# 144 sixteen-bit products ahead of a down projection, and casts among the up projection, in a two-layer trunk on one core

## The chip, the cores and the metric

The kernel runs on one core of one Trainium2 chip. The time is device microseconds of one launch, the median of several runs. Beside it there is a trace of one execution, taken by the hardware profiler.

## The reference

Two layers over 256 frames of width 1024, each an attention mixer and then a PEER mixer with a layer norm behind each. Layer 0's attention is multi-head latent attention, layer 1's selects 64 keys per query. The change lies in the PEER mixer of layer 0. It picks 16 of 16384 experts for each token and head, and mixes them:

```python
s1 = einsum('thd,hnd->thn', q[:, :, 0], sub_keys[0]);  s2 = ...q[:, :, 1], sub_keys[1]
v1, i1 = top_k(s1, 16);  v2, i2 = top_k(s2, 16)
best, pos = top_k(v1[..., :, None] + v2[..., None, :], 16)   # experts = pairs of keys
gate = softmax(best)
u = w_down[expert];  a = einsum('td,ted->te', x, u)
y = einsum('te,ted->td', gelu(a) * gate, w_up[expert])
x = layernorm(ALPHA * x + y)
```

## The kernel before, in words

The kernel doesn't gather experts. It multiplies all 256 tokens with all 16384 rows of the down table, 128 blocks of 128 experts each, applies gelu, multiplies by a gate that is zero except at the chosen experts, and multiplies the result with all 128 blocks of the up table. Each 32-bit operand is split into a part `hi` and a rest `lo` (the weights) or `xh` and `xl` (the activations), and each product is three: hi with xh, hi with xl, lo with xh.

**The weight stream** (class `Stream`). SyncE loads a block of 128x1024 into one of four `raw` buffers (L101). ScalarE casts it to `hi` (L119), VectorE subtracts to get `lo` (L123; on GpSimd at L121 for some blocks). `hi` and `lo` go into rings of four blocks (`RING = 4`), so a cast waits until TensorE has used the block four before it, and a load waits until the subtraction has freed its buffer.

**`peer(li)`** runs for each layer. `queries` and `scores` make the queries (products `pq`) and their scores against the keys (products `ps`, 32-bit, 128 wide). While they and the first part of the down stage run, `choose` does the top-16 steps on VectorE, dealt out in portions between the products. `gates` ends it, with four transposes on TensorE (`gT`, L1056).

*The down stage* is the loop over `b0`: two blocks per turn, each of 24 products `d` with 256 columns, out of a pool of four PSUM buffers (`ps(...)`, the pool `psp`); ScalarE applies gelu. From the point where the gates are ready, each turn also has `prepare` (16-bit one-hot tables on VectorE L1119, GpSimd L1121 and ScalarE L1125) and `place`, 16 products `G` of 16 bits and 128 columns.

*The up stage* is the loop over `k`: 128 blocks, each of 12 products `y` with 512 columns into four PSUM banks that stay open to the end. Before every second block `operand` splits the activations into `xh` (ScalarE, L1182) and `xl` (VectorE, L1183). At `k == 64` the code asks for the loads of the residual `x` and of the norm's gain and bias, into places of the arena `A` whose activations have been used. `finish` takes the last four blocks and the norm.

All matmuls but the transposes are issued by one helper, so they bear line L277. The tables `iotac` (50x16 entries) and `iota4` (128x4), both 16-bit and filled with small whole numbers, are made at the start; the function `first` already multiplies `iotac` with a 16-bit `iota16`, into a PSUM tile `idle` that nobody reads (L1219), before the first weights have landed.

**What sets the order.** The framework's scheduler puts the instructions of each engine into one fixed order, by a simulation of its own; `chains` and `issue_after` hold some of them in the written order. On the chip each engine takes its queue strictly in that order.

Of the kernel before, what the change touches and what calls it, by code (L numbers as in the profile page):

```python
# [12 lines left out]
F16 = mybir.dt.float16  # L13
U32 = mybir.dt.uint32
AF = mybir.ActivationFunctionType
ALU = mybir.AluOpType
AX = mybir.AxisListType

P = 128
T = 256  # L20
D = 1024
# [162 lines left out]
def tile_trunk(ctx: ExitStack, tc: tile.TileContext, ins, out: bass.AP):  # L184
    nc = tc.nc
# [18 lines left out]
    def ps(name):  # L204
        return psp.tile([P, 512], F32, tag="ps", name=name)
# [15 lines left out]
    iota4 = const.tile([P, P, 4], F16, tag="iota4", name="iota4")  # L221
    iotac = const.tile([P, CELLS, TOPK], F16, tag="iotac", name="iotac")
# [84 lines left out]
    def load_x(ar, src):  # L307
        xs = [ar.take(D), ar.take(D)]
        for t in range(2):
            nc.sync.dma_start(xs[t], src[t])  # L310
        return xs
# [203 lines left out]
    def load_affine(ar, li, which):  # L515
        g, b = ar.take(D), ar.take(D)
        nc.sync.dma_start(g, ins["ln_gain"][li, which].partition_broadcast(P))
        nc.sync.dma_start(b, ins["ln_bias"][li, which].partition_broadcast(P))
        return g, b
# [421 lines left out]
    def peer(li):  # L941
# [186 lines left out]
        def place(g4, done):  # L1128
# [10 lines left out]
            if done:  # L1139
                nc.vector.scalar_tensor_tensor(A[:, :done, tsl], pv[:, :done, :], 1.0 / GSCALE, A[:, :done, tsl],  # L1140
                                               op0=ALU.mult, op1=ALU.mult)

        groups = prepared = 0
        ready = False
        for b0 in range(0, NKEYS, 2):
            p = ps(f"d{b0}")
# [26 lines left out]
        lnar = Arena(arena)  # L1173
# [15 lines left out]
        for k in range(NKEYS - STAGGER):  # L1189
            rows(y4, operand(k), ws.get(), k == 0, False)  # L1190
            if k == 64:
                x = load_x(lnar, keep)
                g, b = load_affine(lnar, li, 1)
        spare = [lnar.take(D) for _ in range(5)]

        finish(y4, operand, NKEYS, g, b, x, spare, None if last else lead_values)

# [66 lines left out]

    mla()
    peer(0)
    dsa()
    peer(1)


# [71 lines left out]
```

## Time and profile before

| | us |
|---|---|
| median of the runs | 1798.12 |
| the two runs | 1797.7 and 1798.54 |
| profiled execution | 1797.2 |
| its span in the trace | 1795.4 |
| down stage of layer 0, from 145.07 to | 529.41 |
| up stage of layer 0, from 529.41 to | 877.60 |
| granted TensorE clock, mean | 0.999 |

The page of the profile has the busy time of each engine and the chain that ended last, followed back from the last instruction. The view of groups has, for each kind of instruction, its count, busy time, the mean time of one, and the idle time ahead of it with what ended it. PE is TensorE, PEld its weight loads, DVE VectorE, ACT ScalarE, POOL GpSimd, SP SyncE. Matmuls overlap in the trace, so the time that one more costs is the distance between starts, which the chain gives as a piece's length over its count.

### The profile page before, as it was taken

The numbers are of one execution on the slowest core, as the hardware profiler recorded it, in microseconds if no ns is written. First come the engines' busy times: TensorE is split into PE (matmuls) and PEld (weight loads), VectorE is DVE, ScalarE is ACT, GpSimd is POOL, SyncE is SP. The second block draws the span as 40 slices with busy tenths as digits, with TensorE's granted clock in tenths as the row PEclk, the third lists the DMA queues.
The fourth block names the chain that finished last, engine by engine and source line by source line (L and its number), as shares of the span: only waits on it lengthen the run. The fifth ranks groups of instructions, "written<-read, shape, count | busy, mean of one in ns | idle before, by whom it ended". The sixth has DMA issues, their size and how long they took to land.

```text
span 1795.4 us, 32370 instructions
## 1 busy us (share of the span) xinstructions
PE 1784.0 (99%) x12495; PEld 1631.1 (91%) x12495; DVE 1336.2 (74%) x2319; ACT 1053.2 (59%) x1832; POOL 406.2 (23%) x288
## 2 busy tenths in 40 slices
PE   9999999999999999999999999999999999999998
PEld 8899999999998888888889899999999988888886
DVE  6688998888985555555688789997889865555555
ACT  6655545888864444444467554557888754444443
POOL 2012354555520000000023013544555400000000
PEclk9999999999999999999999999999999999999999
DMA  6555556444556565655646455565454476565553
GB/s 233 211 175 179 189 200 194 159 165 165 165 188 222 190 198 191 196 191 196 205 164 225 172 173 185 192 200 177 165 164 162 157 246 197 190 197 190 196 191 118
DMA packets 93468, 335.47 MB, mean 187 GB/s; under 512 B 10368, under 2 KB 11392, under 8 KB 93312
## 3 DMA queue, kind: packets, MB, share of 16 engines
q1 hardware_dynamic: 93024, 332.87, 56.0%
q8 instruction: 98, 1.61, 0.3%
q14 instruction: 58, 0.48, 0.1%
q10 hardware_dynamic: 288, 0.52, 0.1%
HBM read 329.16 MB, written 4.19 MB: 186 GB/s over the span
## 4 chain that ended last, share of the span: by engine, by line
PE 98%; DVE 1%; issue 0%; DMA 0%; ACT 0%; POOL 0%; SPq 0%; DVEq 0%; POOLq 0%; ACTq 0%
PE y L277 41%; PE d L277 39%; PE pq L277 4%; PE G L277 3%; PE q L277 3%; PE v L277 1%; PE qw L277 1%; PE s L277 1%; PE ps L277 1%; PE h L277 1%; PE qi L277 1%; PE o L277 1%; PE qn L277 0%; DMA raw<-in_mla_h 0%; PE pt L280 0%
## 5 line engine op out<-in xcount | busy, mean ns | idle before, releaser
L123 DVE TENSOR_TENSOR lo<-raw,hi 128x1024 fp32r<-128x1024 f32 (+1 forms) x556 | 747.5, 1346 | 289.5 <-ACT hi L119 288.0
L119 ACT CAST hi<-raw 128x1024 fp32r<-128x1024 f32 (+1 forms) x583 | 611.0, 1049 | 522.8 <-PE d L277 222.4
L277 PE MATMUL d<-xh,hi 128*128 128x256 f32 x2048 | 572.9, 280 | 0.0
L277 PE MATMUL d<-xh,lo 128*128 128x256 f32 x2048 | 566.8, 277 | 0.0
L277 PE MATMUL d<-xl,hi 128*128 128x256 f32 x2048 | 566.8, 277 | 0.0
L277 PEld LDWEIGHTS d<-xh,lo 128*128 128x128 f32 x2048 | 385.2, 188 | 0.0
L277 PEld LDWEIGHTS d<-xh,hi 128*128 128x128 f32 x2048 | 384.9, 188 | 0.0
L277 PEld LDWEIGHTS d<-xl,hi 128*128 128x128 f32 x2048 | 384.7, 188 | 0.0
L277 PE MATMUL y<-hi,xh 128*128 128x512 f32 x1088 | 337.8, 390 | 0.0
L277 PE MATMUL y<-lo,xh 128*128 128x512 f32 x1088 | 337.7, 389 | 0.0
L277 PE MATMUL y<-hi,xl 128*128 128x512 f32 x1088 | 337.2, 389 | 0.0
L1121 POOL TENSOR_TENSOR gate<-hot,gate 128x512 f16<-128x512 f16 x128 | 220.5, 1741 | 214.4 <-DVE hot L1119 214.4
L277 PEld LDWEIGHTS y<-lo,xh 128*128 128x128 f32 x1088 | 204.1, 188 | 42.8 <-DVE lo L123 0.3
L277 PEld LDWEIGHTS y<-hi,xl 128*128 128x128 f32 x1088 | 204.2, 188 | 42.4
L277 PEld LDWEIGHTS y<-hi,xh 128*128 128x128 f32 x1088 | 203.8, 188 | 41.9
L371 POOL TENSOR_TENSOR st<-st,mhalf 128x1 f32<-128x1 f32 x8 | 4.4, 550 | 802.1 <-DVE st L369 802.1
L1125 ACT ACTIVATE gate<-hot,rest 128x128 f16<-128x128 f16 x512 | 165.9, 411 | 1.1 <-DVE hot L1119 1.0
L1182 ACT CAST xh<-arena 128x512 fp32r<-128x512 f32 x128 | 79.7, 623 | 145.5 <-PE y L277 145.3
L1183 DVE TENSOR_TENSOR xl<-arena,xh 128x512 fp32r<-128x512 f32 x128 | 88.2, 692 | 72.7 <-ACT xh L1182 72.7
L121 POOL TENSOR_TENSOR lo<-raw,hi 128x1024 fp32r<-128x1024 f32 x27 | 65.2, 2414 | 218.4 <-ACT hi L119 213.1
L1119 DVE TENSOR_TENSOR hot<-iota,place 128x1024 f16<-128x1024 f16 x128 | 85.7, 709 | 32.3 <-PE G L277 32.2
L1043 POOL TENSOR_TENSOR arena<-arena 128x800 f32<-128x800 f16 x32 | 71.0, 2229 | 58.1 <-DVE arena L1040 58.1
(220 smaller groups left out, 1803.5 us busy)
## 6 DMA issues: line engine op xcount, KB each, us to landing
raw<-in_down SPq DMA_DIRECT2D x256, 512.0 KB, 3.3
raw<-in_up SPq DMA_DIRECT2D x256, 512.0 KB, 4.3
raw<-in_peer_q SPq DMA_DIRECT2D x24, 512.0 KB, 4.2
raw<-in_dsa_qk SPq DMA_DIRECT2D x16, 512.0 KB, 3.4
raw<-in_mla_w_o SPq DMA_DIRECT2D x8, 512.0 KB, 5.6
arena<-in_peer_q SPq DMA_DIRECT2D x8, 512.0 KB, 5.1
raw<-in_dsa_v SPq DMA_DIRECT2D x8, 512.0 KB, 4.4
raw<-in_dsa_w_o SPq DMA_DIRECT2D x8, 512.0 KB, 4.3
```

Source lines behind the costliest of these rows:

```text
L119: self.act(lambda: nc.scalar.copy(hi, raw))
L121: nc.gpsimd.tensor_tensor(lo, raw, hi.bitcast(F32), op=ALU.subtract)
L123: self.dve(lambda: nc.vector.tensor_tensor(lo, raw, hi.bitcast(F32), op=ALU.subtract))
L277: return pe(lambda: nc.tensor.matmul(o, l, r, start=start, stop=stop, skip_group_check=True))
L371: nc.gpsimd.tensor_tensor(st[:, 5:6], st[:, 4:5], mhalf, op=ALU.pow)
L1043: nc.gpsimd.tensor_tensor(o.rearrange("p k c -> p c k"), same, cell[t][:, h, :, None].to_broadcast([P, CELLS, TOPK]), op=ALU.mult)
L1119: nc.vector.tensor_tensor(hot, iota4[:, None].to_broadcast([P, 2, P, 4]), place16[:, :, None, four].to_broadcast([P, 2, P, 4]), op=ALU.is_ ...
L1121: nc.gpsimd.tensor_tensor(gate[:, 0], hot[:, 1].rearrange("p c j -> p j c"), gate16[:, four, None].to_broadcast([P, 4, P]), op=ALU.mult)
L1125: nc.scalar.mul(gate[:, 1, j, :], hot[:, 1, :, j], rest[:, t : t + 1])
L1182: nc.scalar.copy(hh, a)
L1183: nc.vector.tensor_tensor(al, a, hh.bitcast(F32), op=ALU.subtract)
```

## The change

Two insertions, both for layer 0 only. The first puts 144 products with their own weight loads ahead of the down loop: 96 with 256 columns and 48 with 512, from the tables `iotac` (as weights, at eight offsets) and `iota4`, into a PSUM tile `spin` out of the pool of four. Nobody reads it. The second puts five instructions into the up loop, three times: a 16-bit scaled copy of `x[0]` on ScalarE, the remainder on VectorE, the same again with a sum, and a scaled copy and a remainder on GpSimd. They write to the places `spare`, which `finish` uses later for the norm; `spare` is now taken at `k == 64` instead of behind the loop, at the same addresses.

```diff
+        if li == 0:
+            flat = iotac.rearrange("p c k -> p (c k)")
+            wide4 = iota4.rearrange("p k j -> p (k j)")
+            spin = ps("spin")
+            for width, count in ((256, 96), (512, 48)):
+                for i in range(count):
+                    nc.tensor.matmul(spin[:, :width], flat[:, 80 * (i % 8) : 80 * (i % 8) + P],
+                                     wide4[:, :width], start=True, stop=True)
+
         groups = prepared = 0
         ready = False
         for b0 in range(0, NKEYS, 2):
...
             if k == 64:
                 x = load_x(lnar, keep)
                 g, b = load_affine(lnar, li, 1)
-        spare = [lnar.take(D) for _ in range(5)]
+                spare = [lnar.take(D) for _ in range(5)]
+            if k in (80, 84, 88) and li == 0:
+                hi16, lo16 = spare[0].bitcast(F16)[:, :D], spare[1].bitcast(F16)[:, :D]
+                nc.scalar.mul(hi16, x[0], 1024.0)
+                nc.vector.scalar_tensor_tensor(lo16, x[0], 1024.0, hi16, op0=ALU.mult, op1=ALU.subtract)
+                nc.vector.scalar_tensor_tensor(lo16, x[0], 1024.0, hi16, op0=ALU.mult, op1=ALU.subtract,
+                                               accum_out=spare[2][:, 0:1])
+                nc.gpsimd.tensor_scalar(lo16, x[0], 1024.0, None, op0=ALU.mult)
+                nc.gpsimd.tensor_tensor(lo16, x[0], hi16, op=ALU.subtract)
```

Apart from the insertions the order of every engine is the same as before, but for one place: the second half of the last score products. Before, TensorE's queue has it inside the first down block. Here are the last rows of that stretch, before the change (`d` is the first down block):

```order
L277 MATMUL d_1570<-xh,hi 128x256
L277 MATMUL d_1570<-xl,hi 128x256
L277 MATMUL ps_1558<-arena 128x128 x2
L277 MATMUL ps_1564<-arena 128x128 x2
L277 MATMUL d_1570<-xh,lo 128x256
```

With the change the same four products stand among the new ones, behind 26 of them, as they stood behind 26 of `d`:

```order
L1149 LDWEIGHTS iotac
L1149 MATMUL spin<-iota_99,iotac 128x256
L277 MATMUL ps_1558<-arena 128x128 x2
L277 MATMUL ps_1564<-arena 128x128 x2
L1149 LDWEIGHTS iotac
```

The first down block comes behind the last of the 144. In the queue of VectorE the casts' instructions stand between the subtractions `lo` and `xl` of the up stage, among the early blocks, and not where the code asks for them; the second of the three looks so (`raw_7331` to `raw_7383` are blocks 23 to 26):

```order
L123 TENSOR_TENSOR lo<-raw_7331,hi 128x1024
L123 TENSOR_TENSOR lo<-raw_7349,hi 128x1024
L1207 SCALAR_TENSOR_TENSOR arena<-arena 128x1024
L1192 TENSOR_TENSOR xl<-arena,xh 128x512
L1208 SCALAR_TENSOR_TENSOR arena<-arena 128x1024
L123 TENSOR_TENSOR lo<-raw_7365,hi 128x1024
L123 TENSOR_TENSOR lo<-raw_7383,hi 128x1024
```

Before, the same stretch is two `lo`, one `xl`, two `lo`. In ScalarE's queue the added instruction stands right behind the cast of block 24, with the next `xh` and `hi` casts behind it:

```order
L119 CAST hi<-raw_7349 128x1024
L1206 ACTIVATE arena<-arena 128x1024
L1191 CAST xh<-arena 128x512
L119 CAST hi<-raw_7365 128x1024
L119 CAST hi<-raw_7383 128x1024
```

From the second time on this instruction waits for GpSimd to be done with the time before.

## The prediction

> **What bounds the kernel now.** I read the totals of the engines first, then the chain that ended last, then what TensorE waited for.
>
> ```profile
> PE 1784.0 (99%) x12495; PEld 1631.1 (91%) x12495; DVE 1336.2 (74%) x2319; ACT 1053.2 (59%) x1832; POOL 406.2 (23%) x288
> PE 98%; DVE 1%; issue 0%; DMA 0%; ACT 0%; POOL 0%; SPq 0%; DVEq 0%; POOLq 0%; ACTq 0%
> ```
>
> The first row is busy time by engine. The second is the share of each engine in the chain that ended last. TensorE carries 98% of the chain, so time added to its queue should come out at the end unless TensorE was waiting where it is added. The waits of the matmuls are these, in all:
>
> ```profile
> PE idle L1219 <- DVE iotac L230: 2.5, 1, 2.5
> PE qw L277 <- DVE xl L402: 0.6, 2, 0.3
> PE o L277 <- ACT arena L592: 0.3, 1, 0.3
> PE wi L280 <- ACT arena L864: 0.3, 1, 0.3
> ```
>
> Columns are total, count and longest in us. Together that is 3.7 us, 2.5 of it ahead of the first matmul, and none is in layer 0's channel mixer. The chain around the place of the change is closed:
>
> ```profile
> 139.99 4.20 PE pq L277 x37
> 144.18 0.89 PE ps L277 x8
> 145.07 2.96 PE d L277 x26
> 148.03 0.89 PE ps L277 x8
> 148.92 154.83 PE d L277 x1366
> 303.76 0.43 PE gT L1056 x4
> 304.19 11.31 PE d L277 x96
> 315.50 0.93 PE G L277 x16
> ...
> 529.41 348.19 PE y L277 x1536
> ```
>
> Columns are start, length, what, and how many (the last row is from the same view of the up stage). Each piece starts where the one before ends. The d products, 256 columns wide, come every 154.83 / 1366 = 113.3 ns; the y products, 512 wide, every 348.19 / 1536 = 226.7 ns; the 16-bit G products, 128 wide, every 0.93 / 16 = 58 ns. These intervals, not the longer "mean ns of one" (280 or 390), are what one more product costs, since each overlaps the next.
>
> **The products.** 96 are 256 wide, 48 are 512 wide, all 16-bit, each with its own weight load. They add a rate times a count, and no other engine reads them. The nearest row of their own kind is the warm-up at the start, 16-bit and 512 wide from nearly the same tables:
>
> ```profile
> 2.50 4.00 PE L1219 MATMUL idle<-iotac,iota 128*128 128x512 f16 x9 [2.50 <-DVE iotac L230]
> 6.30 0.94 PE L277 MATMUL h<-xh,hi 128*128 128x256 f32 x4
> ```
>
> Nine take 6.30 - 2.50 = 3.80 us, 422 ns each, about twice what the y products take later at the same width. So the array runs these first products at half rate. Three prices follow.
>
> Half of 422 is 211 ns for 512 columns and 105.6 for 256: 96 x 0.1056 + 48 x 0.211 = 10.1 + 10.1 = 20.3 us. This is the low end. The d and y rows give 96 x 0.1133 + 48 x 0.2267 = 10.9 + 10.9 = 21.8 us. The G row, scaled by width (116 and 232 ns), gives 11.1 + 11.1 = 22.3 us, the high end; a G product is so short that its own weight load must fit into 58 ns, which the wider products need not mind. I take **21.0 us**, between the first two (the first is 16-bit but from a cold array, the second warm but 32-bit).
>
> What of it lies beside other work? The order shows that the second half of the last score products (ps) keeps its cover: before, 26 d products stood between the two halves; now 26 of the new products do, 26 x 0.11 = 2.9 us against 2.96. So the copy of the queries that these products wait for is covered as before, and nothing is gained there. The stream of weights doesn't stand still for free either: its ring of four blocks fills within a few microseconds, then ScalarE, VectorE and the DMAs stop until TensorE frees a slot. They resume with a full ring, as they would have had. VectorE's chain of top-16 steps is queued in one order with the ring's subtractions, so it stops too; it gets at most a few steps ahead, and TensorE waits for that chain nowhere (the piece of four gate transposes, 0.43 us, joins the d products on both sides). One tile more from the four PSUM buffers shifts the buffers of the d blocks by one; the buffer it takes was emptied blocks before. All this I cost at nothing; if the gates were late after all, d would stop at 303.76, where the chain shows no stop today.
>
> **The casts.** Three times the up stage of layer 0 gains one ScalarE, two VectorE and two GpSimd instructions over 128x1024. The code asks for them at blocks 80, 84 and 88, but the order has them as early as their operands allow: the ScalarE instruction behind the casts of blocks 13, 24 and 28, some 557 to 603 us into the trace. None feeds TensorE, but all stand in the queues that feed it.
>
> ```profile
> L123 DVE TENSOR_TENSOR lo<-raw,hi 128x1024 fp32r<-128x1024 f32 x125 | 153.2, 1226 | 105.9 <-ACT hi L119 105.9
> L119 ACT CAST hi<-raw 128x1024 fp32r<-128x1024 f32 x125 | 131.3, 1051 | 101.8 <-PE y L277 101.8
> L1183 DVE TENSOR_TENSOR xl<-arena,xh 128x512 fp32r<-128x512 f32 x63 | 43.5, 692 | 36.6 <-ACT xh L1182 36.6
> L1182 ACT CAST xh<-arena 128x512 fp32r<-128x512 f32 x61 | 38.0, 624 | 72.7 <-PE y L277 72.7
> ...
> L364 DVE SCALAR_TENSOR_TENSOR arena<-arena,st 128x1024 f32<-128x1024 f32 x8 | 10.3, 1282 | 0.2
> L121 POOL TENSOR_TENSOR lo<-raw,hi 128x1024 fp32r<-128x1024 f32 x27 | 65.2, 2414 | 218.4 <-ACT hi L119 213.1 <-PE pt L280 5.3
> L1121 POOL TENSOR_TENSOR gate<-hot,gate 128x512 f16<-128x512 f16 x128 | 220.5, 1741 | 214.4 <-DVE hot L1119 214.4
> ...
> raw<-in_up SPq DMA_DIRECT2D x256, 512.0 KB, 4.3
> ```
>
> The first four rows are from the stretch 529.5 to 877.5, the next three from the whole run, the last is the load of a block with its median time to landing. A block is 348.19 / 128 = 2.72 us of TensorE; four blocks are 10.88. In four blocks VectorE has 4 x 1.226 + 2 x 0.692 = 6.29 us of work, and gets 2 x 1.28 = 2.56 more: 8.85. ScalarE has 4 x 1.051 + 2 x 0.624 = 5.45, and gets one of about 1.05: 6.50. Both fit. There is also a lead: the hi casts' idle time ends at "PE y", that is, the ring is full and a cast starts when a slot comes free, three blocks (8.16 us) before the block is needed. Less 1.05 and 1.23 us for cast and subtraction, 5.88 us are to spare. Behind the subtraction also waits the load of the block four later, into the buffer that it frees: 1.05 + 1.23 + 4.3 = 6.6 of the 10.88 us until that block's cast, another 4.3 to spare.
>
> Queued behind the added ScalarE instruction are the hi and xh casts, and from the second time on it waits for GpSimd. A full-width GpSimd subtraction took 2.41 us; twice the 512-wide 16-bit one is 3.48. So GpSimd needs 4.8 to 7.0 us each time. The tightest turn is from block 24 to 28. While ScalarE does its added instruction, VectorE does a subtraction (1.23), then the two added ones with an xl between (2 x 1.28 + 0.69), then GpSimd its 4.8 to 7.0: 9.3 to 11.5 us in all, and the next ScalarE instruction is due after 10.88. ScalarE waits at most 0.6 us, well under the 5.88. What GpSimd does to VectorE beside it is seen in the down stage:
>
> ```profile
> 336.20 3.44 POOL L1121 TENSOR_TENSOR gate<-hot,gate 128x512 f16<-128x512 f16 x2 [3.01 <-DVE hot L1119]
> 336.64 2.08 DVE L123 TENSOR_TENSOR lo<-raw,hi 128x1024 fp32r<-128x1024 f32 x1
> ```
>
> The subtraction takes 2.08 us there against 1.226 alone, 0.85 more. With three such in four blocks VectorE needs 8.85 + 2.6 = 11.4 us, 0.6 more than it has, so 1.7 us behind after three rounds, out of the lead of 5.88. I cost the casts at **0**. Without that cover they would cost up to 9 us (below).
>
> The Trainium skill (SBUF — State Buffer, "Who interferes with whom") has a harsher rule: a VectorE instruction with two SBUF inputs and a GpSimd instruction that reads SBUF exclude each other for the whole instruction. By that rule VectorE stands for all the time of GpSimd; the row of 2.08 us neither proves nor excludes it, since two GpSimd instructions overlap it, and the time by it would be the third rival's.
>
> **The sum.** The profiled execution took 1797.2 us (span 1795.4 and 1.8 around it): 1797.2 + 21.0 + 0 = 1818.2. The median of the runs, 1798.12, is 0.9 above that execution, so I predict **1819 us**, 1.2% slower. About 2% either way, 1762 to 1834, is what a measurement of this kernel can tell from no change; this stays inside it.
>
> **Rivals.**
>
> First, *half rate*: the new products run as the warm-up did, 0.211 us per 256 columns and 0.422 per 512. That is 96 x 0.211 + 48 x 0.422 = 40.5 us, 1839 us, over the 2% line. For it: 16-bit products of 512 columns have only been seen at that rate. It decides from 15 us more than I take, when some three quarters of the products run so. Against it: the warm-up began on an idle array, while here over 100 us of products run ahead of it, and the G products hold 58 ns for 128 columns, full rate, right between d products. The granted clock doesn't separate the two cases:
>
> ```profile
> 2.50:6.30 3.80, 3.80 (x10) 1.00 1.02 395
> 148.92:303.75 154.83, 154.83 (x1369) 1.00 0.59 192
> ```
>
> It is 1.00 (the column ahead of the DMA share) in both. I give it 4%. The Trainium skill (TensorE: Matmul & The Clock Gate, Part 1) ties the half rate to an array that was idle for a window of about 3.4 us, not to the operands. By that rule the new products run at full rate, and the time is 1818 to 1820.
>
> Second, *no cost*: the products vanish because nothing reads them, or fill time in which TensorE waits. Then the kernel takes 1798 us, not slower than before. For it: PSUM tile "spin" is never read. Against it: the "idle" products are never read either and are in the trace, and the chain has no gap at this place to fill. 2%.
>
> Third, *the casts break the stream*: VectorE stands while GpSimd works. Per four blocks that is 8.85 + 4.8 to 7.0 = 13.7 to 15.9 us against 10.88, 2.8 to 5.0 behind each time, 8.4 to 15 after three, less the lead of 5.88: TensorE waits 2.5 to 9 us between blocks 20 and 35. It decides as soon as GpSimd takes over 4 us a round. 1821.5 to 1828 us. For it: the subtraction of 2.08 us. Against it: GpSimd and VectorE were both at work in the down stage, and d never stopped. 8%.
>
> **How the numbers follow.** The forecast has 86%. Its own range is 20.3 to 22.3 us of products, 1818 to 1821. The third rival's lower part is taken in, and a microsecond or two below for products that overlap better than any row shows: **1816 to 1825**. Slower by over 2% is the first rival and a rest that I can't name: 0.05. Faster by over 2% would need a gain of 36 us where TensorE waits 3.7 us in all: 0.01. Within 2%: 0.94.
>
> **What would show it.** In the changed profile a group "spin" of 144 products with some 21 us from first to last start, the d products at 113 ns behind it, y at 226.7 ns throughout, and everything after the products later by that amount. In the up stage some of VectorE's subtractions of blocks 20 to 33 stretched toward 2 us beside GpSimd, and no wait of y. The forecast is wrong if the products take over 25 us, if y waits for "lo" or "hi" by over 3 us, or if the d and y intervals themselves move.

## The result and the profile after

The changed kernel takes 1818.37 us (two runs, 1817.97 and 1818.76) against 1798.12: a ratio of 1.0114, with a 95% interval of 1.0098 to 1.0131. That is 20.25 us more, where 20.9 were forecast; 1819 was predicted, in a range of 1816 to 1825.

Here is the chain that ended last in the changed kernel, around the place of the products. Columns are start, length, what, how many:

```profile
144.10 0.89 PE ps L277 x8
144.99 2.84 PE spin L1149 x26
147.83 0.89 PE ps L277 x8
148.73 18.00 PE spin L1149 x118
166.73 157.78 PE d L277 x1392
324.51 0.44 PE gT L1056 x4
324.94 11.31 PE d L277 x96
...
550.16 348.19 PE y L277 x1536
```

The products are a closed piece of the chain, cut only by the score products, as the order had it. 26 of 256 columns take 2.84 us, 109.2 ns each. Of the other 118, 70 are of 256 columns, 70 x 0.1092 = 7.64 us, which leaves 10.36 / 48 = 215.8 ns for one of 512. Together 2.84 + 18.00 = 20.84 us. A kernel with the wide products first (below) shows that width by itself: there the 22 ahead of the score products take 4.75 us, 215.9 ns each. Behind them nothing has changed its rate: d has 157.78 / 1392 = 113.3 ns as before, y has the same 348.19 us for its 1536. The y piece begins 550.16 - 529.41 = 20.75 us later, and the span is 1816.2 against 1795.4, 20.8 longer.

What TensorE waited for, in all (total in us, times, longest):

```profile
PE idle L1236 <- DVE iotac L230: 2.5, 1, 2.5
PE qw L277 <- DVE xl L402: 0.6, 2, 0.3
PE o L277 <- ACT arena L592: 0.3, 1, 0.3
PE h L277 <- ACT xh L1240: 0.3, 1, 0.3
PE wi L280 <- ACT arena L864: 0.3, 1, 0.3
PE h L277 <- DVE xh L1240: 0.2, 1, 0.2
```

There is no wait of y. The casts do show in the queues that feed it. From VectorE's timeline of the changed kernel, beside the first two rounds (start, length, line, instruction, what it had waited for):

```profile
602.99 1.47 DVE L123 TENSOR_TENSOR lo<-raw,hi 128x1024 fp32r<-128x1024 f32 x1 [0.51 <-ACT hi L119]
...
605.77 3.05 DVE L123 TENSOR_TENSOR lo<-raw,hi 128x1024 fp32r<-128x1024 f32 x1
...
619.30 1.67 DVE L123 TENSOR_TENSOR lo<-raw,hi 128x1024 fp32r<-128x1024 f32 x1 [1.43 <-ACT hi L119]
```

The same from GpSimd and ScalarE:

```profile
601.50 3.61 POOL L1210 TENSOR_SCALAR arena<-arena 128x1024 f16<-128x1024 f32 x1 [65.37 <-DMA raw<-in_up]
605.19 2.54 POOL L1211 TENSOR_TENSOR arena<-arena 128x1024 f16<-128x1024 f32 x1
612.92 3.68 POOL L1210 TENSOR_SCALAR arena<-arena 128x1024 f16<-128x1024 f32 x1 [5.19 <-DVE arena L1208]
616.69 3.20 POOL L1211 TENSOR_TENSOR arena<-arena 128x1024 f16<-128x1024 f32 x1
```

```profile
619.92 1.06 ACT L1206 ACTIVATE arena<-arena 128x1024 f16<-128x1024 f32 x1 [0.65 <-POOL arena L1211]
```

Beside GpSimd's first instruction a subtraction takes 1.47 us, beside its second, from 605.77 on, 3.05 instead of 1.23: it ends about one subtraction's time after GpSimd's instruction, which ends at 605.19 + 2.54 = 607.73. The two GpSimd instructions don't act alike: the subtraction of 1.47 us begins and ends while the first one, the scaled copy from 601.50 to 605.11, is under way. At 619.30 VectorE has again waited 1.43 us for a cast, as in the undisturbed blocks ahead: the lead is back, and TensorE has seen nothing. The third ScalarE instruction waits 0.65 us for GpSimd.

### The profile page after: what moved, and what is told of

It reads as the page before. It is cut to its first block, busy times and chain, and to the rows that moved or that the text cites. A ratio compares the mean times of both kernels' runs of the same rounds, so it can differ in the third digit from the quotient of the medians.

```text
span 1816.2 us, 32683 instructions
## 1 busy us (share of the span) xinstructions
PE 1804.2 (99%) x12639; PEld 1645.0 (91%) x12639; DVE 1346.9 (74%) x2328; ACT 1056.1 (58%) x1835; POOL 426.0 (23%) x294
## 4 chain that ended last, share of the span: by engine, by line
PE 98%; DVE 1%; issue 0%; DMA 0%; ACT 0%; POOL 0%; SPq 0%; DVEq 0%; POOLq 0%; ACTq 0%
PE y L277 40%; PE d L277 39%; PE pq L277 4%; PE G L277 3%; PE q L277 3%; PE v L277 1%; PE spin L1149 1%; PE qw L277 1%; PE s L277 1%; PE ps L277 1%; PE h L277 1%; PE qi L277 1%; PE o L277 1%; PE qn L277 0%; DMA raw<-in_mla_h 0%
```

## The experiments

**The parts alone.** Four kernels on the same chip: the products without the casts, the casts without the products, the products twice, and a harder press on VectorE. The first leaves out the cast lines, the second the block that makes the products. All kernels but the second are without the casts, also where the edit shown doesn't say so. The first three were run several times; each of the others ran once, and what those show is read from their rows and not from a microsecond in their times.

```diff
-            if k in (80, 84, 88) and li == 0:
...
-                nc.gpsimd.tensor_tensor(lo16, x[0], hi16, op=ALU.subtract)
```

> The 144 products without the casts of the up stage. Theory (the products are the whole cost, the casts are hidden in the lead of the weight ring): the same time as the changed kernel, 1818 us within 1, that is 20 to 21 us over the kernel before; 26 products of 256 columns in 2.84 us and the remaining 118 in 18.0 us as in the changed kernel. Rival (the casts take part of the 20 us): 1810 to 1817 us, and an up stage shorter than 348.2 us against the changed kernel's.

Measured: 1818.64 us, ratio 1.0116 (1.0099 to 1.0133), 26 products in 2.84 us and 118 in 18.00. The same as the changed kernel.

```diff
-        if li == 0:
...
-                                     wide4[:, :width], start=True, stop=True)
```

> The three rounds of casts without the products. Theory: 1798 us within 1, no difference from the kernel before; ScalarE's third added instruction waits about 0.6 us for GpSimd, and the y products keep 226.7 ns. Rival (VectorE stands while GpSimd works): 1800.5 to 1807 us, with waits of y for lo in blocks 20 to 35.

Measured: 1797.94 against 1797.75 us, ratio 1.0001 (0.9991 to 1.0011), y in 348.19 us without a wait. So the casts cost less than 0.11%, 2 us, and by the chain nothing; the rival that gave them a share falls.

```diff
-            for width, count in ((256, 96), (512, 48)):
+            for width, count in ((256, 192), (512, 96)):
```

> 288 products (192 of 256 columns, 96 of 512) and no casts. Theory (the price is a rate times a count): 2 x 20.8 = 41.7 us over the kernel before, 1840 us, with 109.2 and 215.8 ns each from the first to the last. Rival (a longer stretch of 16-bit products is slowed, or the ring that fills in the meantime buys something back): above 1843 or below 1837 us, and the rate of the second half differs from that of the first.

The chain of that kernel, start, length, what and how many:

```profile
144.99 2.84 PE spin L1149 x26
...
148.72 38.84 PE spin L1149 x262
```

Measured: 1839.34 us, ratio 1.0233 (1.0216 to 1.0250), 41.6 over the kernel before. The products take 2.84 + 38.84 = 41.68 us, twice 20.84. The price is a rate times a count; a pause of 42 us in the weight stream neither costs nor buys anything more.

**How far the cover for the casts reaches.** In place of the casts there are instructions that keep GpSimd and VectorE at work together:

```diff
+            if 80 <= k < 120 and k % 2 == 0 and li == 0:
+                lo16 = spare[1].bitcast(F16)[:, :D]
+                nc.vector.scalar_tensor_tensor(lo16, x[0], 1024.0, x[1], op0=ALU.mult, op1=ALU.subtract)
+                for _ in range(2):
+                    nc.gpsimd.tensor_tensor(spare[3], x[0], x[1], op=ALU.subtract)
```

> No products; in place of the three rounds of casts, 20 VectorE subtractions over 128x1024 and 40 GpSimd subtractions over 128x1024 in the up stage, with nothing between them to wait for, so that GpSimd is at work without a break. The sums that they write are not part of the reference's computation. Per two blocks (5.44 us) VectorE has 2 x 1.23 + 0.69 + 2 x 1.22 = 5.6 us of work if GpSimd leaves it alone. Three theories. No slowing: 0.15 us behind per two blocks, all in the lead of 5.9 us, 1798 to 1800 us. Slowing by 0.85 us for each VectorE instruction with two SBUF inputs (2.08 against 1.23 in the trace of before), some 3.9 us per two blocks: 4.1 behind, 41 after ten pairs of blocks, less the lead: y waits for lo some 35 us, about 1833 us. Exclusion for the whole instruction, VectorE and GpSimd taking turns: five GpSimd instructions of 2.4 us between VectorE's five, 12 us behind per two blocks, over 1900 us.

From this kernel, TensorE's longest wait (total, times, longest), then VectorE's and GpSimd's timelines some 70 us into the up stage:

```profile
PE y L277 <- DVE lo L123: 43.4, 18, 6.3
```

```profile
598.23 3.43 DVE L1197 SCALAR_TENSOR_TENSOR arena<-arena 128x1024 f16<-128x1024 f32 x1
601.59 3.43 DVE L123 TENSOR_TENSOR lo<-raw,hi 128x1024 fp32r<-128x1024 f32 x1
604.94 3.42 DVE L1197 SCALAR_TENSOR_TENSOR arena<-arena 128x1024 f16<-128x1024 f32 x1
608.27 2.87 DVE L1183 TENSOR_TENSOR xl<-arena,xh 128x512 fp32r<-128x512 f32 x1
611.07 3.36 DVE L123 TENSOR_TENSOR lo<-raw,hi 128x1024 fp32r<-128x1024 f32 x1
```

```profile
597.26 22.72 POOL L1199 TENSOR_TENSOR arena<-arena 128x1024 f32<-128x1024 f32 x7 [80.78 <-DVE xl L1183]
```

Measured: 1862.77 us against 1797.75 (a single run of it), 65 more. None of the three forecasts hit the time, but the rows decide on the mechanism. In this stretch every VectorE instruction takes 2.8 to 3.4 us, its own work of 0.69 or 1.23 included, and GpSimd's come every 22.72 / 7 = 3.25 us: the two take turns, one instruction each. My figure for that case, over 1900, let the turns go on for all ten pairs of blocks at five a pair. GpSimd had only 40 instructions, and was done by 724.5 us; and the added VectorE instructions were through at 665.7, after which only three instructions a pair took turns, 9.4 us a pair instead of 16.0. Of the 65 us, 43.4 are waits; most of the rest is that the products behind each wait come at half rate (below). The middle theory, a fixed 0.85 us for each instruction, falls: xl pays over 2 us for 0.69 of work.

```diff
-                for _ in range(2):
-                    nc.gpsimd.tensor_tensor(spare[3], x[0], x[1], op=ALU.subtract)
+                for _ in range(4):
+                    nc.gpsimd.memset(spare[3], 0.0)
```

> As the kernel with 20 VectorE and 40 GpSimd subtractions, but GpSimd fills 80 times a place of 128x1024 with zeros, which reads nothing; no products. The places are not part of the reference's computation. Theory (VectorE and GpSimd take turns only where both read the on-chip memory): VectorE's instructions keep 1.23 and 0.69 us, 1798 to 1800 us. Rival (any GpSimd instruction that writes there takes turns with VectorE): some 40 us or more over the kernel before, with waits of y for lo.

The groups of this kernel between 550 and 700 us (count, busy time, mean ns of one, idle time ahead):

```profile
L1199 POOL MEMSET arena<- 128x1024 f32 x80 | 76.5, 956 | 85.3 <-DVE xl L1183 80.8
L123 DVE TENSOR_TENSOR lo<-raw,hi 128x1024 fp32r<-128x1024 f32 x56 | 68.6, 1224 | 31.8 <-ACT hi L119 31.8
L1197 DVE SCALAR_TENSOR_TENSOR arena<-arena 128x1024 f16<-128x1024 f32 x20 | 24.4, 1220 | 0.0
L1183 DVE TENSOR_TENSOR xl<-arena,xh 128x512 fp32r<-128x512 f32 x28 | 19.3, 691 | 11.6 <-ACT xh L1182 11.6
```

Measured: 1797.93 us, no difference from 1797.79. With GpSimd at work for 76.5 us but reading nothing, VectorE's instructions keep 1.22 and 0.69 us. So GpSimd's writing alone doesn't make VectorE take turns, and its subtraction, which reads, does. The Trainium skill (SBUF — State Buffer, "Who interferes with whom") states both halves of this, and both runs agree. Reading alone isn't the whole of it: GpSimd's scaled copy in the changed kernel reads too, and beside it VectorE's subtractions took 1.47 to some 2 us and ended before it did. It has one input where the subtraction has two; no run here says whether that is why.

**What sets the rate of a product.** First the same 144 from 32-bit operands:

```diff
-            flat = iotac.rearrange("p c k -> p (c k)")
-            wide4 = iota4.rearrange("p k j -> p (k j)")
+            flat = xl.rearrange("p c t -> p (c t)")
+            wide4 = xh.rearrange("p c t -> p (c t)")
```

> The same 144 products at the same place, but from 32-bit operands (slices of xl as weights, of xh as the moving side), and no casts. If the d and y intervals (113.3 and 226.7 ns) belong to the 32-bit type: 96 x 0.1133 + 48 x 0.2267 = 21.8 us for the 144, 1.0 more than the 16-bit ones. If the type doesn't matter and the d and y stages are slowed by other work (casts, loads): 109.2 and 215.8 ns, 20.8 us.

The chain of that kernel:

```profile
145.85 3.08 PE spin L1149 x26
...
149.82 19.39 PE spin L1149 x118
```

Measured: 1820.53 us against 1798.0. 118.5 ns for 256 columns, and (19.39 - 70 x 0.1185) / 48 = 231 ns for 512: 22.5 us, 1.6 more than 16-bit. With 32-bit operands a product is dearer, by more than the d and y rows say (113.3 and 226.7 ns). The operands' contents and places differ too in this run; the type is the difference that it was made for, and the others weren't tried alone.

Then the products at the very start, in place of the nine warm-up products:

```diff
-        busy(WARM, 512)
+        wide4 = iota4.rearrange("p k j -> p (k j)")
+        for width, count in ((256, 96), (512, 48)):
+            for i in range(count):
+                queue("pe", lambda: nc.tensor.matmul(idle[:, :width], some[:, 80 * (i % 8) : 80 * (i % 8) + P],
+                                                     wide4[:, :width], start=True, stop=True))
```

> The 144 products stand at the very start in place of the nine warm-up products of 512 columns, and no casts. The first weights are there some 6 us into the trace, so about 3.8 us of the products fill a wait. If the half rate belongs to an array that has just been idle: about 3.8 us at 211 ns for 256 columns (some 18 products), then 109 and 216; first to last start about 22.7 us, and the kernel some 19 us over the kernel before. If the half rate belongs to 16-bit products of these tables: 211 and 422 ns to the end, 40 us, and about 37 us over the kernel before.

The chain of that kernel, at its start:

```profile
2.50 23.62 PE idle L1255 x144
26.13 0.47 PE h L277 x4
```

Measured: 1815.33 us against 1798.0. The 144 take 23.62 us, 2.8 more than at full rate. At 211 instead of 109.2 ns that is some 27 products, 5.8 us, at half rate and the rest at full rate. The trace has the change near 8 us. Here are two stretches of it (from and to in us, length, TensorE's busy time and its products in brackets, those under way at an edge counted in, then the granted clock and two columns on the DMAs):

```profile
7.00:8.00 1.00, 1.00 (x7) 1.00 1.00 401
8.00:10.00 2.00, 2.00 (x21) 1.00 1.01 411
```

The kernel is 17.3 us longer, near the 19 of the first theory and far from the 37 of the second. The same products run at both rates, so the half rate belongs to the array that starts from rest and not to these operands, and it lasts longer than the 3.8 us I read from the nine. The pressed kernel shows it in mid-run. There, behind a wait of 4.62 us, the products from 615.26 to 617.82 (two to a row) come at 427 ns each, and full rate is back some 3.3 us behind the wait. Half rate sets in once more behind a wait of 2.02 us:

```profile
614.48 0.98 PE L277 MATMUL y<-lo,xh 128*128 128x512 f32 x2 [4.62 <-DVE lo L123]
615.26 1.05 PE L277 MATMUL y<-hi,xl 128*128 128x512 f32 x2
616.12 1.05 PE L277 MATMUL y<-hi,xh 128*128 128x512 f32 x2
...
617.82 0.81 PE L277 MATMUL y<-hi,xl 128*128 128x512 f32 x2
618.47 0.63 PE L277 MATMUL y<-hi,xh 128*128 128x512 f32 x2
621.11 0.81 PE L277 MATMUL y<-lo,xh 128*128 128x512 f32 x2 [2.02 <-DVE lo L123]
621.72 1.06 PE L277 MATMUL y<-hi,xl 128*128 128x512 f32 x2
622.57 1.06 PE L277 MATMUL y<-hi,xh 128*128 128x512 f32 x2
```

The same columns in narrow products:

```diff
-            for width, count in ((256, 96), (512, 48)):
+            for width, count in ((128, 384),):
```

> The same number of columns in 384 products of 128 columns (16-bit, in the place of the 144), and no casts. If each product costs its columns at the full rate and a fixed 2.5 ns (109.2 - 106.7 and 215.8 - 213.3): 55.8 ns each, 21.4 us. If the G products' 58 ns is what a weight load takes: 58 ns each, 22.3 us.

The chain of that kernel:

```profile
145.11 1.79 PE spin L1149 x32
...
147.84 19.65 PE spin L1149 x352
167.50 164.00 PE d L277 x1392
```

The products behave as the first theory said: 1.79 / 32 and 19.65 / 352, 55.8 to 55.9 ns each, 21.44 us. But the kernel takes 1825.17 us, 27.2 more. The rest is in the next row: d takes 164.00 us for the same 1392, 117.8 ns each instead of 113.3, with no wait anywhere. The rate of d depends on what ran before it. Two runs ask why:

```diff
+            for width, count in ((128, 384), (512, 2)):
```

> The 384 products of 128 columns, with two of 512 columns behind them, and no casts. Behind the narrow products alone the d products came every 117.8 ns instead of 113.4 up to the gates, 6.2 us in all. Theory one (narrow products leave TensorE's weight loads without a lead, and the d products, whose own loads take as long as they do, never win it back; a wide product gives the loads time to get ahead): d at 113.4 ns behind the two wide ones, some 21.4 + 0.4 = 21.9 us over the kernel before. Theory two (the number of instructions or their place in memory sets it): d stays at 117.8 ns, about 28 us over the kernel before.

The down stage in the chain of that kernel:

```profile
168.76 157.78 PE d L277 x1392
```

Measured: 1820.0 us against 1797.79. Two wide products behind the narrow ones bring d back to 157.78 us. The number of instructions is not the cause, for this kernel has two more.

```diff
+            for width, count in ((512, 48), (256, 96)):
```

> The 144 products of the change with the 48 wide ones first and the 96 of 256 columns last, no casts. If a product of 256 columns (109 ns) leaves the 16-bit weight loads enough time: no difference, 20 to 21 us over the kernel before and d at 113.4 ns. If only 512 columns give the loads a lead: d at 117.8 ns, some 27 us over the kernel before.

The first products and the down stage in the chain of that kernel:

```profile
145.71 4.75 PE spin L1149 x22
...
167.44 157.78 PE d L277 x1392
```

Measured: 1818.85 us, d in 157.78. 256 columns are enough. That the narrow products use up the lead of the weight loads fits all three, but no view shows the lead itself, so it stays an explanation and isn't shown.

## Why the prediction was right

**The bound.** That TensorE's chain is closed at this place, so that time added there comes out at the end, held to 0.1 us in the two traces: 20.84 us of products, 20.8 of span. So close a fit of the spans is partly luck, since the spans of the kernel before alone lie between 1795.4 and 1796.9 us; the y piece, which begins 20.75 us later, says the same from inside the run.

**The rate.** 21.0 us was a choice between 20.3 (half of the cold 16-bit row) and 21.8 (the warm 32-bit rows); it measured 20.84. That the pick came within 0.2 us was in part luck: no row of the kernel before has 16-bit products of these widths in a warm array, and the bounds were what the rows gave. Half of the cold row is too cheap, 211 ns against 215.8; the d and y rows are too dear, and their operands are 32-bit. The G row, taken for the high end, was bound otherwise: a warm 16-bit product of 128 columns takes 55.8 ns, and G's 58 is above it by something that these runs don't name. The Trainium skill (TensorE: Matmul & The Clock Gate, "Back-to-back issue gap") gives N / 2.4 + 2.5 ns for N columns in a warm array; that is 55.8, 109.2 and 215.8 for the three widths, which is what was measured, and by that line the forecast would have been 20.8 us. But the same section calls this the gap of an isolated product and gives about 81 ns for 128 columns and about 131 ns for 512 in a sustained stream of weight loads and products; here, with a weight load for each product, the stream took 55.8 and 215.8 ns.

**The cover of the score products** held: they stand behind 26 products, in 2.84 us, and TensorE did not wait for the copy ahead of them.

**The casts.** Zero was right, and the lead of 5.9 us was the right reason. The pressed kernel lets its size be estimated: when TensorE first waited, for 4.62 us, VectorE had lost about 2.2 us in each of five turns, 11 us, so some 6 us had gone unseen. Two sizes inside it: GpSimd's pairs took 6.2 to 7.0 us from start to end, within the 4.8 to 7.0; ScalarE waited 0.65 us where at most 0.6 was worked out. What failed is the reading of the 2.08 us row as a fixed 0.85 us for each subtraction. Beside GpSimd's subtraction the two engines take turns, as the third rival said of the mechanism: one VectorE subtraction took over 3 us there, not the 2 that were to show. The rival's price did not come about, because it let VectorE stand through all of each GpSimd pair, while in fact VectorE went on beside the first of the two, held up by at most some 0.8 us at a time, and had caught up by 619.30. With 40 turns in a row it comes about: y waited 43.4 us.

**The half rate** was right to be held off: an idle array sets it, the operands don't. That the granted clock doesn't separate the two cases was a wrong reading. In the kernel before, the trace's record of the clock begins only 6.81 us into the span, and a stretch without a record reads 1.00, so the 1.00 of the first products says nothing of them; in the kernel with the products at the start it begins at 7.88, close to where the rate changes. In mid-run the column does show the half rate. First 50 us of the pressed kernel (TensorE busy, weight loads, VectorE, ScalarE, GpSimd, then the clock, 0.78), then TensorE alone in two stretches of 3.4 us, the first of them with the slow products behind 614.48:

```profile
600.00:650.00 50.00, 30.90 (x100) 23.30 (x99) 50.00 (x17) 10.66 (x12) 48.75 (x17) 0.78 0.19 70
614.80:618.20 3.40, 3.40 (x9) 0.50 0.42 154
618.20:621.60 3.40, 1.38 (x6) 1.00 0.00 0
```

**No cost** was wrong as thought: products that nobody reads are carried out, in full.

## What to carry to other kernels

Where the chain that ended last is one engine without gaps, work added to that engine costs its interval times its count, and the interval is to be taken from rows of the same operand type and width, length over count of a chain piece, not from the mean time of one. It can also change the rate of what comes behind it, as the narrow products did, so look at that row too. Work on the engines that feed it is free as long as its stalls stay within the lead of the ring; count that lead in microseconds, and where GpSimd subtracts beside VectorE, count turns of one instruction each.

## What the runs showed of the hardware that was not expected

TensorE's rate for the same instructions has more than one steady value. The down stage ran its 1392 products at 113.3 ns behind wide products and at 117.8 behind 352 narrow ones, for 160 us, without any wait in the trace, and two products of 512 columns ahead of it brought the fast value back. A single stretch of narrow products so cost 6 us beyond its own time. The piece of 96 behind the gate transposes has 11.31 / 96 = 117.8 ns in the kernel before, too. Why the rate has two values isn't shown.
